# A macaron decoder trunk: the third conv group's products ahead of the scores, its taps behind the groups' maxima, the output projection begun between the last groups

## The chip, the cores and the metric

The kernel runs on one core of one Trainium2 chip. The metric is the device time of one execution in microseconds (us). The engines are TensorE (PE; PEld is its weight load), VectorE (DVE), ScalarE (ACT), GpSimd (POOL) and SyncE (SP, which issues the loads). Matmuls write to PSUM, of which the kernel has eight banks of 128 x 512 floats: three under the tag `mm`, one `cf`, two `po`, two `pt`.

## The reference

Two layers over 512 tokens of width 1024, all in float32. Each layer is a half-step SwiGLU (inner width 2816), a mixer, a second half-step SwiGLU and a norm. The change is in the mixer alone:

```python
n = rms_norm(h, mix_norm[l])
p = n @ w_in[l]
u_conv, q, k, v, q_mem = jnp.split(p, splits, axis=-1)
y_conv = conv_module(u_conv, ...)   # GLU, causal depthwise conv of 31 taps, LayerNorm, silu: 384 channels
y_swa = sliding_window_attention(q, k, v, sinks)   # 6 heads, window 128, blocks of 128, learned sinks
y_mem = memory_attention(qm, mk, mv)   # 4 heads over 256 memory tokens
y = jnp.concatenate([y_conv, y_swa, y_mem], axis=-1)
h = h + y @ w_out[l]
```

q, k and qm are normed a head; q and k are rotated.

## The kernel before, in words

Activations lie with channels on the partitions, as tiles of 128 x 512. Every large product is made of three matmuls in a rounded format, hi*hi + lo*hi + hi*lo (`mm3`, lines 174 to 176), so each weight tile is first split into a rounded half `hi` and the rest `lo`. `weights` does that in one of two ways. With VectorE: ACT copies the loaded tile `raw` to `hi` (L143) and VectorE subtracts (L144). With POOL (`split_by_dma`): ACT makes `hi` (L148) and `-hi` (L149), and an accumulating DMA that POOL issues adds the weights to it from memory (L150). There are three `raw` buffers and four pairs of `whi` and `wlo`; `spare()` gives another place, the pair of a gated tile.

The mixer of a layer, in the order of the string ORDER:

- `conv_half(c, i)`, steps c00 to c21: the products of conv group c (three groups of 128 channels), i = 0 the values and i = 1 the gates. VectorE scales them by R, the spread of the token norms (L665, L668), ACT takes the sigmoid (L669), VectorE multiplies (L670) into `ypad`.
- `queries(t)`, q0 to q3, one block of 128 tokens each, with norms and rotation on ACT (L684, L537), POOL (L689) and VectorE; `query_columns(t)`, Q0 to Q3, transposes them. `values(t)`, v0 to v3, makes the values and the memory queries, which ACT copies out (L711, L713) and squares (L537); `value_columns(t)`, V0 to V3, transposes the memory queries.
- `attention`, step a, works through ten groups (GROUPS) of up to three head pairs, "r" for memory heads, "w" for window heads. `scored` makes the scores of a group on PE (L741 the mask, L747) and their maxima on VectorE (L751 or L765), and scales these to a bias (L752 or L766 and L767). `turned` takes the exponentials on ACT (L777), transposes them on PE (L783) and copies them back (L785); `weighted` multiplies by the values on PE (L794); `scaled` divides (L803 to L808); `attended` transposes the result (L817) and splits it. The scores of group n + 1 are issued ahead of the exponentials of group n.
- `taps(c)`, t0 to t2: 31 VectorE instructions a group (L871 once, L874 thirty times), one after another on the same 128 x 512 sums. They come last in ORDER, and the scheduler puts them where VectorE is free.
- `swish`, step s: POOL adds the three groups' sums (L880, L881), PE makes their mean (L883), VectorE subtracts it (L886), ACT squares, PE adds up the squares (L200), VectorE and POOL take the root (L206, L191), PE spreads it over the partitions (L213), and norm and silu follow (L891, L892).
- The output projection: eight tiles of 128 output channels, each from five tiles of attention rows (three of the window heads, two of the memory heads) and three of conv rows. First the five of each, 15 matmuls a tile, then the conv rows, 9 a tile, whose weights are called `ours`; h is updated (L922).

Each engine runs its instructions in order. What that order is, a scheduler decides ahead of time: it takes instructions as they are written here, and picks by its own model of time what an engine does next. `queued()` binds a PE instruction behind the PE instruction that was last put in `tail`, so that PE's order within the mixer is the written one; `tc.issue_after` does the same behind any instruction named. Neither is a wait at run time.

Of the kernel before, what the change touches and what calls it, by code (L numbers as in the profile page):

```python
# [18 lines left out]
P = 128  # L19
# [26 lines left out]

ORDER = "c00 c01 q0 c10 q1 c11 Q0 q2 v0 Q1 q3 v1 Q2 v2 v3 Q3 V0 V1 c20 V2 V3 a t0 t1 t2 s"

# [13 lines left out]
def trunk(ctx: ExitStack, tc: tile.TileContext, xT, memT, pos, w1a, w3a, w2a, w1b, w3b, w2b,  # L62
# [549 lines left out]
    def mixer(l, x, st, last):  # L612
# [28 lines left out]
        def spare():  # L641

            return tuple(z.rearrange("p i s -> p (i s)") for z in gated_pair())

        def conv_half(c, i):
            nonlocal R
            ps = bank([P, S], "po") if c == 2 else mm()
            with queued():
                project(ps, weights(wconv[l, c, i], 1024, V if c + i < 2 else G, spare() if c == 2 else None), x)
            if c == 0:  # L650
                with queued():
                    if i == 0:
                        V.tensor_copy(rc, rms_cols(st, D))
                    else:
                        R = kept(spread(rc), "R", V)
            halves.append((c, i, ps))
            while halves and R is not None:
                gate(*halves.pop(0))
# [17 lines left out]
        def queries(t):  # L676
# [19 lines left out]
            per_head(q[:, CCH:], rq[:, t, NH:], 2)  # L696

        def query_columns(t):
            with queued():
                pt = to_columns(qT[:, :, blk(t)], query[t // 2][:, t % 2], 4)  # L700
            A.activation(kT[:, blk(t)], pt[:, CC, :], AF.Copy, scale=HD**-0.5)
# [29 lines left out]
        def scored(kind, pairs):  # L731
# [17 lines left out]
            if not masked:  # L749
                for i in range(2):  # L750
                    V.tensor_reduce(out=nmr[:, b, i], in_=pp[i], axis=AX.X, op=ALU.max)  # L751
                V.scalar_tensor_tensor(out=nmr[:, b], in0=nmr[:, b], scalar=-1.0, in1=by_half(rm[:, b, :]), op0=ALU.mult, op1=ALU.mult)  # L752
                return pp, W
# [12 lines left out]
            V.scalar_tensor_tensor(out=at_(nmw), in0=at_(nmw), scalar=-1.0, in1=rr, op0=ALU.mult, op1=ALU.mult)  # L766
            V.tensor_tensor(out=at_(nmw), in0=at_(nmw), in1=per(nsinks), op=ALU.min)  # L767
            G.tensor_tensor(out=at_(esw), in0=at_(nmw), in1=per(sinks), op=ALU.add)
            return pp, W

        def turned(kind, b, c, scores, W):
# [3 lines left out]
            for i in range(2):  # L775
                n = 2 * c + i
                A.activation(pr[:, i, 0:W], scores[i], AF.Exp, bias=nm[:, b, i, c : c + 1], scale=rr[:, b, n : n + 1])  # L777
            nk = W // P
# [32 lines left out]
        def attended(kind, b, z):  # L811
# [7 lines left out]
            while c < n:  # L819
# [6 lines left out]
        GROUPS = (("r", (0, 0), (0, 1)), ("r", (1, 0), (1, 1)), ("w", (0, 0), (0, 1), (0, 2)), ("w", (1, 0), (1, 1)), ("w", (2, 0), (2, 1)),  # L826
                  ("w", (1, 2), (2, 2)), ("r", (2, 0), (2, 1)), ("w", (3, 0), (3, 1)), ("w", (3, 2)), ("r", (3, 0), (3, 1)))

        def attention():
# [17 lines left out]

            s = scored(GROUPS[0][0], GROUPS[0][1:])
            conv_half(2, 1)
            yy.extend([gated_pair() for _ in range(KD // 2)][::-1])  # L850
            y.extend(at(p, ALL, i, ALL) for p in yy for i in range(2))
            for n, (kind, *pairs) in enumerate(GROUPS):
                ready = list(done)
                done.clear()
                nxt_s = None
                if n + 1 < len(GROUPS):
                    nxt_s = scored(GROUPS[n + 1][0], GROUPS[n + 1][1:])
                for z, (b, c) in enumerate(pairs):
                    x = turned(kind, b, c, [ps[:, z, :] for ps in s[0]], s[1])
                    close()  # L860
                    late = (kind, b, c, *x)
                s = nxt_s
                for r in ready:
                    attended(*r)
            close()
            for r in done:
                attended(*r)


        def taps(c):  # L870
            V.tensor_scalar(out=cv[:, c, :], in0=ypad[:, c, 0:S], scalar1=conv_w[:, c, 0:1], scalar2=conv_b[:, c : c + 1],  # L871
                            op0=ALU.mult, op1=ALU.add)
            for j in range(1, TAPS):
                V.scalar_tensor_tensor(out=cv[:, c, :], in0=ypad[:, c, j : j + S], scalar=conv_w[:, c, j : j + 1],  # L874
                                       in1=cv[:, c, :], op0=ALU.mult, op1=ALU.add)

# [17 lines left out]

        for step in ORDER.split():
            f = {"c": conv_half, "q": queries, "Q": query_columns, "v": values, "V": value_columns, "a": attention, "t": taps,
                 "s": swish}[step[0]]
            f(*map(int, step[1:]))


        oo = []
        for d in range(KD):
            w = weights(wout[l, d, :, CCH:], 640, G if d < 4 else V)
            ps = bank([P, S], ("mm", "mm", "mm", "cf", "po", "po", "pt", "pt")[d])
            for n in range(5):
                mm3(ps, at(w, ALL, blk(n)), y[CC + n], n == 0, False)
            oo.append(ps)

# [141 lines left out]
```

## Time and profile before

| what | us |
|---|---|
| three runs, median | 1813.62 |
| lowest and highest of them | 1808.96 and 1815.8 |
| the profiled execution | 1811.26 |
| its span in the profile | 1809.1 |
| PE busy in the span | 1767.9 |
| VectorE busy | 1281.7 |
| ACT busy | 897.4 |
| layer 0's mixer, first conv gate to first output product | 397.0 to 507.4 |
| layer 1's, the same | 1290.7 to 1399.9 |

Times inside a profile are counted from the start of its span. A row of the timeline has the start, the duration, the engine, the line, the operation, output and inputs, and in brackets the idle time of the engine just before, with what ended it. A row of a stretch has the busy time of each engine in it with the count of instructions, the clock that PE was granted (1.00 is full), the busy share of the DMA engines, and GB/s.

### The profile page before, as it was taken

The page shows a single profiled execution, that of the slowest core. Times are in us where ns is not written, and L with a number is a line of the kernel's source. Part 1 is how long each engine was busy: PE and PEld are TensorE (multiplying, and loading weights), DVE is VectorE, ACT ScalarE, POOL GpSimd, SP SyncE. Part 2 cuts the span into 40 slices and gives each one's busy share as a digit, 9 for nine tenths or more (in the row PEclk, how much of TensorE's full clock was granted, in tenths as well). Part 3 has the DMA queues.
Part 4 walks back from the last instruction along what each step waited for, and adds up shares of the span by engine and source line. Part 5 has one row for each costly group of instructions (what it writes and reads, how often), then busy time and mean ns, then how long its engine had stood idle before and what let it go on. Part 6 is the DMA issues. An engine that isn't in the chain of part 4 may idle for free.

```text
span 1809.1 us, 28077 instructions
## 1 busy us (share of the span) xinstructions
PE 1767.9 (98%) x10996; PEld 1585.8 (88%) x10996; DVE 1281.7 (71%) x1896; ACT 897.4 (50%) x1357; POOL 189.0 (10%) x207
## 2 busy tenths in 40 slices
PE   8999999999899999999999999999989999999997
PEld 6989999888688989898888898988877889898986
DVE  7969666569957857575678685766698567675755
ACT  5546444464655535353655463535456645453532
POOL 3001000025001000000010010000340010000000
PEclk9999999999899999999999999999999999999998
DMA  9466655275039456465556465643640666474622
GB/s 274 107 168 173 177 131 150 55 203 114 2 104 206 111 143 172 135 167 138 155 137 156 145 174 142 172 120 94 162 104 1 182 139 162 129 182 121 168 80 82
DMA packets 93589, 250.44 MB, mean 138 GB/s; under 512 B 9617, under 2 KB 11921, under 8 KB 93457
## 3 DMA queue, kind: packets, MB, share of 16 engines
q1 hardware_dynamic: 77040, 190.45, 34.9%
q0 software_dynamic: 16416, 58.20, 17.8%
q8 instruction: 86, 1.41, 0.3%
q14 instruction: 47, 0.38, 0.1%
HBM read 246.52 MB, written 2.10 MB: 137 GB/s over the span
## 4 chain that ended last, share of the span: by engine, by line
PE 79%; DVE 11%; issue 6%; ACT 2%; DMA 2%; SPq 0%; POOLq 0%; DVEq 0%; POOL 0%; ACTq 0%
PE mm L174 10%; PE mm L176 10%; PE mm L175 10%; PE po L176 9%; PE po L174 9%; PE po L175 9%; PE pt L174 6%; PE pt L175 6%; PE pt L176 6%; DVE there L874 6%; DMA raw<-in_wvm 1%; DVE wlo L144 1%; PE po L794 1%; DVE nmw L765 1%; ACT uu L777 0%
## 5 line engine op out<-in xcount | busy, mean ns | idle before, releaser
L143 ACT ACTIVATE whi<-raw 128x1024 fp32r<-128x1024 f32 (+3 forms) x360 | 337.9, 941 | 487.0 <-PE mm L175 235.7
L144 DVE TENSOR_TENSOR wlo<-raw,whi 128x1024 fp32r<-128x1024 f32 (+3 forms) x352 | 380.1, 1081 | 145.1 <-ACT whi L143 143.6
L175 PE MATMUL mm<-glo,whi 128*128 128x512 f32 x752 | 293.6, 391 | 0.0
L174 PE MATMUL mm<-ghi,whi 128*128 128x512 f32 x752 | 290.5, 391 | 0.7 <-ACT ghi L143 0.7
L176 PE MATMUL mm<-ghi,wlo 128*128 128x512 f32 x734 | 285.6, 389 | 0.0
L176 PE MATMUL po<-mh,wlo 128*128 128x256 f32 x864 | 244.6, 283 | 1.1 <-DVE wlo L144 1.1
L174 PE MATMUL po<-mh,whi 128*128 128x256 f32 x864 | 244.7, 283 | 0.2 <-ACT part L386 0.2
L175 PE MATMUL po<-ml,whi 128*128 128x256 f32 x864 | 244.5, 283 | 0.0
L176 PE MATMUL pt<-xhi,wlo 128*128 128x256 f32 x864 | 244.0, 283 | 0.0
L175 PE MATMUL pt<-xlo,whi 128*128 128x256 f32 x864 | 243.9, 283 | 0.0
L174 PE MATMUL pt<-xhi,whi 128*128 128x256 f32 x864 | 243.0, 283 | 0.3 <-ACT xhi L143 0.3
L464 DVE SCALAR_TENSOR_TENSOR h<-mm,h 128x512 f32<-128x512 f32 x128 | 87.7, 688 | 138.1 <-PE mm L176 138.1
L174 PEld LDWEIGHTS mm<-ghi,whi 128*128 128x128 f32 x752 | 141.2, 188 | 30.3 <-ACT ghi L143 1.2
L176 PEld LDWEIGHTS po<-mh,wlo 128*128 128x128 f32 x864 | 165.8, 192 | 1.3 <-DVE wlo L144 1.3
L174 PEld LDWEIGHTS po<-mh,whi 128*128 128x128 f32 x864 | 165.8, 192 | 1.2 <-ACT part L386 0.4
L175 PEld LDWEIGHTS pt<-xlo,whi 128*128 128x128 f32 x864 | 165.7, 192 | 0.8
L175 PEld LDWEIGHTS po<-ml,whi 128*128 128x128 f32 x864 | 165.8, 192 | 0.6
L174 PEld LDWEIGHTS pt<-xhi,whi 128*128 128x128 f32 x864 | 165.1, 192 | 1.4 <-ACT xhi L143 0.5
L175 PEld LDWEIGHTS mm<-glo,whi 128*128 128x128 f32 x752 | 141.3, 188 | 28.3 <-issue 0.5
L176 PEld LDWEIGHTS pt<-xhi,wlo 128*128 128x128 f32 x864 | 165.6, 192 | 0.0
L176 PEld LDWEIGHTS mm<-ghi,wlo 128*128 128x128 f32 x734 | 137.8, 188 | 29.0 <-issue 0.5
L874 DVE SCALAR_TENSOR_TENSOR there<-ypad,par,there 128x512 f32<-128x512 f32 x180 | 135.5, 764 | 1.4
(314 smaller groups left out, 3305.9 us busy)
## 6 DMA issues: line engine op xcount, KB each, us to landing
raw<-in_w2a SPq DMA_DIRECT2D x48, 384.0 KB, 3.6
raw<-in_w2b SPq DMA_DIRECT2D x48, 384.0 KB, 3.5
raw<-in_w1b SPq DMA_DIRECT2D x26, 512.0 KB, 3.7
raw<-in_w3b SPq DMA_DIRECT2D x26, 512.0 KB, 3.7
raw<-in_w1a SPq DMA_DIRECT2D x25, 512.0 KB, 3.7
raw<-in_w3a SPq DMA_DIRECT2D x25, 512.0 KB, 3.7
wsum<-in_w1a SPq DMA_DIRECT2D x18, 512.0 KB, 4.4
wsum<-in_w3a SPq DMA_DIRECT2D x18, 512.0 KB, 4.3
```

The lines of the kernel that those rows point to most:

```text
L143: A.activation(hi, x, AF.Copy)
L144: on.tensor_tensor(out=lo, in0=x, in1=hi.bitcast(F32), op=ALU.subtract)
L174: T.matmul(ps, a[0], b[0], start=first, stop=False, **more)
L175: T.matmul(ps, a[0], b[1], start=False, stop=False, **more)
L176: tail[0] = T.matmul(ps, a[1], b[0], start=False, stop=last, **more)
L464: added = V.scalar_tensor_tensor(out=h[:, d, :], in0=ps, scalar=0.5, in1=h[:, d, :], op0=ALU.mult, op1=ALU.add)
L765: V.tensor_reduce(out=each(nmw, i), in_=pp[i], axis=AX.X, op=ALU.max)
L794: tail[0] = T.matmul(po[:, 2 * c + i, :], ptb[:, i, j, :], v, start=(j == 0), stop=(j == nk - 1))
L874: V.scalar_tensor_tensor(out=cv[:, c, :], in0=ypad[:, c, j : j + S], scalar=conv_w[:, c, j : j + 1], in1=cv[:, c, :], op0=ALU.mult, op1=AL ...
```

## The change

ORDER becomes `c00 c01 q0 c10 q1 c11 Q0 q2 q3 Q1 c20 c21 Q2 v0 Q3 v1 V0 V1 g0 g1 v2 v3 V2 a t0 t1 t2 s`. The third conv group's products (c20, c21) come ahead of the values and of all scores; the scores of groups 0 and 1 (g0, g1, the new function `begin`) come ahead of v2 and v3; V3 moves into the first group. The weights of v0 to v3 lie in spare pairs, two of the four split by POOL. The taps from the 58th on (EARLY) are bound behind the last step of the groups' maxima, by the counts in LATER. The last three groups change places: the memory heads of block 3 come ahead of the window heads of block 3, and one pair of window heads comes last. The output projection is cut in two functions: `out_weights(d)`, called for the first two tiles ahead of the groups and for the next two inside groups 3 and 5, and `out_rows(d, rows)`, called with the rows of the memory heads (MEMORY) for the first three tiles around the last step of the attention, and with those of the window heads (OWN) after `swish`. `out_rows` issues under `queued()`. The `ours` weights are split by ACT and accumulating DMAs of POOL.

```diff
-ORDER = "c00 c01 q0 c10 q1 c11 Q0 q2 v0 Q1 q3 v1 Q2 v2 v3 Q3 V0 V1 c20 V2 V3 a t0 t1 t2 s"
+ORDER = "c00 c01 q0 c10 q1 c11 Q0 q2 q3 Q1 c20 c21 Q2 v0 Q3 v1 V0 V1 g0 g1 v2 v3 V2 a t0 t1 t2 s"
+EARLY = 58
+LATER = (4, 4, 3, 3, 3, 3, 3, 3, 3, 3)
...
         def conv_half(c, i):
-            ps = bank([P, S], "po") if c == 2 else mm()
+            ps = mm()
-                project(ps, weights(wconv[l, c, i], 1024, V if c + i < 2 else G, spare() if c == 2 else None), x)
+                project(ps, weights(wconv[l, c, i], 1024, V if c + i < 2 else G), x)
...
         def values(t):
-                ww["v"] = [weights(wvm[l, i], 768, V) for i in range(4)]
-            ps = mm()
+                ww["v"] = [weights(wvm[l, i], 768, V if i < 2 else G, spare()) for i in range(4)]
+            ps = mm() if t < 2 else bank([P, S], "po")
...
+        def begin(n):
+            begun[n] = scored(GROUPS[n][0], GROUPS[n][1:])
...
-            s = scored(GROUPS[0][0], GROUPS[0][1:])
-            conv_half(2, 1)
+            for d in range(2):
+                with tc.issue_after(keyed[2].ins):
+                    out_weights(d)
...
+                if final:
+                    for r in ready:
+                        attended(*r)
+                    ready = []
+                elif n + 1 not in begun:
+                    begin(n + 1)
+                if n in (3, 5):
+                    with tc.issue_after(raised[GROUPS[n - 1][0], *GROUPS[n - 1][-1]].ins):
+                        out_weights(len(out_w))
...
+            out_rows(0, MEMORY)
             close()
+            out_rows(1, MEMORY)
+            out_rows(2, MEMORY)
             for r in done:
                 attended(*r)
...
+        OWN, MEMORY = range(CC), range(CC, 5)
+        def out_rows(d, rows):
+            if d == len(oo):
+                oo.append(bank([P, S], ("mm", "mm", "mm", "cf", "po", "po", "pt", "pt")[d]))
+            with queued():
+                for n in rows:
+                    mm3(oo[d], at(out_w[d], ALL, blk(n)), y[CC + n], n == CC, False)
...
             for j in range(1, TAPS):
+                n = c * TAPS + j - EARLY
+                group = sum(n >= sum(LATER[:g]) for g in range(1, len(LATER)))
+                with tc.issue_after(biased[group].ins) if n >= 0 else nullcontext():
...
         for d in range(KD):
+            if d == len(out_w):
+                out_weights(d)
+            out_rows(d, OWN if d < 3 else (*MEMORY, *OWN))
...
-            split(own[0], own[1], raw[:, 0 : 2 * CCH], V)
+            A.activation(own[0], raw[:, 0 : 2 * CCH], AF.Copy)
+            A.activation(own[1], raw[:, 0 : 2 * CCH], AF.Copy, scale=-1.0)
+            for j in range(2):
+                G.dma_start(own[1][:, blk(j, CCH)], wout[l, 2 * i + j, :, 0:CCH], accum_op=ALU.add)
```

How the order of instructions moves is shown at three places of layer 0; numbers behind a name tell tiles apart. Line numbers in the new kernel are higher.

The first is ACT ahead of its first sigmoid. Before, it converts the tiles of c10 (whi_3908), of c11 (whi_3981, wlo_3982) and the first two of the values' weights (128x768):

```order
L143 ACTIVATE whi_3908<-raw_3910 128x1024
L148 ACTIVATE whi_3981<-raw_3983 128x1024
L149 ACTIVATE wlo_3982<-raw_3983 128x1024
L143 ACTIVATE whi_4063<-raw_4065 128x768
L143 ACTIVATE whi_4069<-raw_4071 128x768
L669 ACT_TABLE_LOAD
L669 ACTIVATE aux2_3744<-aux2_3744 128x512
```

Now the tiles of c20 (whi_4112) and c21 (whi_4145) stand there, two copies each:

```order
L151 ACTIVATE whi_3981<-raw_3983 128x1024
L152 ACTIVATE wlo_3982<-raw_3983 128x1024
L151 ACTIVATE whi_4112<-raw_4114 128x1024
L152 ACTIVATE wlo_4113<-raw_4114 128x1024
L151 ACTIVATE whi_4145<-raw_4147 128x1024
L152 ACTIVATE wlo_4146<-raw_4147 128x1024
L675 ACT_TABLE_LOAD
L675 ACTIVATE aux2_3744<-aux2_3744 128x512
```

The values' weights have moved behind the copies of q2.

The second is ACT from its first exponentials to the first copy of turned exponentials (aux0). Before, the sigmoid of c2 stands between them, with table loads:

```order
L777 ACTIVATE uu_3745<-mm_4335,nmr_3754,rm_3751 128x256
L669 ACT_TABLE_LOAD
L669 ACTIVATE aux2_3744<-aux2_3744 128x512
L785 ACTIVATE aux0_3742<-pt_4397 128x512
L785 ACTIVATE aux0_3742<-pt_4405 128x512
L777 ACT_TABLE_LOAD
```

Now the second group's first exponentials and the copies of v2 (po_4313) and v3 (po_4347) stand there:

```order
L786 ACTIVATE pr_3748<-mm_4304,nmr_3754,rm_3751 128x256
L786 ACTIVATE pr_3748<-cf_4305,nmr_3754,rm_3751 128x256
L719 ACTIVATE here_3739<-po_4313,rc_3749 128x2x64
L721 ACTIVATE aux0_3742<-po_4313,rc_3749 128x256
L540 ACTIVATE hsq_4340<-po_4313,rc_3749 128x256
L719 ACTIVATE here_3739<-po_4347,rc_3749 128x2x64
L721 ACTIVATE aux0_3742<-po_4347,rc_3749 128x256
L540 ACTIVATE hsq_4374<-po_4347,rc_3749 128x256
L575 ACTIVATE there_3740<-pt_4381 128x2x128
L786 ACTIVATE uu_3745<-mm_4304,nmr_3754,rm_3751 128x256
L794 ACTIVATE aux0_3742<-pt_4409 128x512
```

The sigmoid of c2 has gone to a place ahead of all exponentials, and the tables change once less often there and back.

The third is PE at the end of the attention. Before, the mean of the conv sums (onesq) stands among the products of the first three output tiles (mm_4957, mm_4980, mm_5003), as the sums of squares and the spread do further on:

```order
L174 MATMUL mm_4957<-ghi_4380,whi_4950 128x512
L174 MATMUL mm_4980<-ghi_4380,whi_4973 128x512
L174 MATMUL mm_5003<-ghi_4380,whi_4996 128x512
L883 MATMUL pt_4906<-aux2_3744,onesq_104 128x512
L175 MATMUL mm_4957<-glo_4381,whi_4950 128x512
L176 MATMUL mm_4957<-ghi_4380,wlo_4951 128x512
```

Now (output tiles mm_4824, mm_4840, mm_4847) they follow one another:

```order
L179 MATMUL mm_4847<-ghi_4399,wlo_4537 128x512
L826 MATMUL pt_4854<-cst_96,aux1_3743 128x128 x3
L928 MATMUL pt_4957<-aux2_3744,onesq_104 128x512
L203 MATMUL cf_4969<-onesq_104,st_4960 128x1 x4
L203 MATMUL cf_4969<-onesq_104,sq_4967 128x1 x4
L216 MATMUL pt_4982<-cst_96,rsq4_4980 128x128 x4
L177 MATMUL mm_4824<-ghi_4403,whi_4385 128x512
```

The 18 products with the memory heads' rows end ahead of them, and every other product of the projection comes behind the spread (L216).

More of the change, by code (lines that the diff above doesn't have):

```diff
@@ L776, in turned @@
                 n = 2 * c + i
-                A.activation(pr[:, i, 0:W], scores[i], AF.Exp, bias=nm[:, b, i, c : c + 1], scale=rr[:, b, n : n + 1])
+                raised[kind, b, c] = A.activation(pr[:, i, 0:W], scores[i], AF.Exp, bias=nm[:, b, i, c : c + 1], scale=rr[:, b, n : n + 1])
             nk = W // P
@@ L873, in taps @@
             for j in range(1, TAPS):
-                V.scalar_tensor_tensor(out=cv[:, c, :], in0=ypad[:, c, j : j + S], scalar=conv_w[:, c, j : j + 1],
-                                       in1=cv[:, c, :], op0=ALU.mult, op1=ALU.add)
+                n = c * TAPS + j - EARLY
+                group = sum(n >= sum(LATER[:g]) for g in range(1, len(LATER)))
+                with tc.issue_after(biased[group].ins) if n >= 0 else nullcontext():
+                    V.scalar_tensor_tensor(out=cv[:, c, :], in0=ypad[:, c, j : j + S], scalar=conv_w[:, c, j : j + 1],
+                                           in1=cv[:, c, :], op0=ALU.mult, op1=ALU.add)
         def swish():
@@ L895, in mixer @@
         for step in ORDER.split():
-            f = {"c": conv_half, "q": queries, "Q": query_columns, "v": values, "V": value_columns, "a": attention, "t": taps,
-                 "s": swish}[step[0]]
+            f = {"c": conv_half, "q": queries, "Q": query_columns, "v": values, "V": value_columns, "g": begin, "a": attention,
+                 "t": taps, "s": swish}[step[0]]
             f(*map(int, step[1:]))
-        oo = []
         for d in range(KD):
[L903 to L907, printed above, removed]
+            if d == len(out_w):
+                out_weights(d)
+            out_rows(d, OWN if d < 3 else (*MEMORY, *OWN))
         more = res.tile([P, 4, 2 * CCH], F32R, tag="nsh", name="whi")
```

24 lines of the change are left out of this document (15 added, 9 removed).

## The prediction

> **What bounds the kernel now.** The page comes first: the run as a whole stands on PE.
>
> ```profile
> span 1809.1 us, 28077 instructions
> PE 1767.9 (98%) x10996; PEld 1585.8 (88%) x10996; DVE 1281.7 (71%) x1896; ACT 897.4 (50%) x1357; POOL 189.0 (10%) x207
> ```
>
> That is an average. The change touches only the mixer, once a layer, so I took the busy time by stretches of layer 0's mixer. After the span of a stretch come PE, PEld, DVE, ACT and POOL, then the granted clock and DMA.
>
> ```profile
> 375.00:380.00 5.00, 4.29 (x19) 2.84 (x17) 2.71 (x4) 5.00 (x8) 1.64 (x2) 1.00 1.04 256
> 380.00:385.00 5.00, 5.00 (x19) 4.15 (x20) 0.91 (x2) 1.74 (x2) 1.93 (x2) 0.66 1.06 274
> 460.00:465.00 5.00, 3.55 (x18) 3.11 (x20) 3.29 (x6) 4.96 (x9) 0.07 (x1) 0.50 0.00 0
> 465.00:470.00 5.00, 5.00 (x33) 4.78 (x31) 3.91 (x10) 1.39 (x4) 0.19 (x1) 0.57 0.00 0
> ...
> 396.98:499.22 102.24, 95.20 (x554) 79.86 (x554) 98.01 (x188) 55.19 (x113) 35.22 (x37) 0.95 0.25 55
> 507.40:555.00 47.60, 47.57 (x221) 39.40 (x222) 28.13 (x43) 28.36 (x41) 4.22 (x5) 1.00 0.63 175
> ```
>
> Three limits follow one another. From the first conv gate (396.98) to the last tap (499.22) VectorE is busy for 98.0 of 102.2 us, so it is the bound there. PE's time between 460 and 470 is at half clock. From 507.4 on PE has no gap at all: the output projection hides everything else.
>
> The timeline of PE shows where it waits in the attention; the bracket is the idle time just before a row.
>
> ```profile
> 461.45 1.97 PE L794 MATMUL po<-mvn,aux 128*128 128x65 f32 x8 [1.77 <-ACT aux L785]
> ...
> 484.91 0.89 PE L783 MATMUL pt<-cst,pr 128*128 128x128 f32 x4 [0.42 <-ACT pr L777]
> 487.23 0.66 PE L783 MATMUL pt<-cst,uu 128*128 128x128 f32 x4 [0.59 <-ACT aux L785]
> 495.03 0.89 PE L783 MATMUL pt<-cst,uu 128*128 128x128 f32 x4 [0.80 <-ACT uu L777]
> 497.16 0.66 PE L783 MATMUL pt<-cst,uu 128*128 128x128 f32 x4 [0.40 <-ACT aux L785]
> 502.70 0.89 PE L783 MATMUL pt<-cst,uu 128*128 128x128 f32 x4 [0.93 <-ACT uu L777]
> 507.43 0.96 PE L174 MATMUL mm<-ghi,whi 128*128 128x512 f32 x3 [0.37 <-ACT ghi L143]
> ```
>
> The last row is the first product of the output projection. The six waits from 484.91 on sum to 3.5 us; PE waits for exponentials whose maxima VectorE reached late, behind taps.
>
> **The change part by part.** *The start of the taps.* ACT runs in order, and before the first sigmoid it converts weights.
>
> ```profile
> 386.93 1.06 ACT L148 ACTIVATE whi<-raw 128x1024 fp32r<-128x1024 f32 x1 [2.71 <-DMA raw<-in_wconv]
> 387.90 1.04 ACT L149 ACTIVATE wlo<-raw 128x1024 fp32r<-128x1024 f32 x1
> 390.53 0.85 ACT L143 ACTIVATE whi<-raw 128x768 fp32r<-128x768 f32 x1 [1.60 <-DMA raw<-in_wvm]
> 393.25 0.85 ACT L143 ACTIVATE whi<-raw 128x768 fp32r<-128x768 f32 x1 [1.87 <-DMA raw<-in_wvm]
> 394.11 1.28 ACT L669 ACT_TABLE_LOAD   x1
> 396.32 0.63 ACT L669 ACTIVATE aux<-aux 128x512 f32<-128x512 f32 x1 [0.92 <-DVE aux L668]
> ```
>
> Two wvm tiles of 384 KB land 2.72 us apart (390.53, 393.25), with the DMA engines full (share 1.04 to 1.06 above). In their place now stand two wconv tiles of 512 KB: 3.63 us each at that rate, so 2 x 0.9 = 1.8 us more. Each takes two copies and not one; only the last tile's count, 2 x 0.97 - 0.85 = 1.1. The 0.92 us for which the sigmoid then waited for VectorE goes, since VectorE no longer has wvm splits ahead of R. Sum +2.0: the taps start at 399.0. PE doesn't wait for it: its next products (q1, c11) stand on banks that VectorE frees with R, ahead of the sigmoid.
>
> *The first maxima.*
>
> ```profile
> 452.97 0.68 DVE L751 TENSOR_REDUCE nmr<-mm 128x2 f32<-128x512 f32 x1
> 455.49 0.15 DVE L752 SCALAR_TENSOR_TENSOR nmr<-nmr,rm 128x4 f32<-128x4 f32 x1
> 457.04 1.93 ACT L777 ACTIVATE uu<-mm,nmr,rm 128x256 f32<-128x256 f32 x4
> 460.82 1.07 ACT L785 ACTIVATE aux<-pt 128x512 f32<-128x512 f32 x2
> L874 DVE SCALAR_TENSOR_TENSOR there<-ypad,par,there 128x512 f32<-128x512 f32 x90 | 67.7, 763 | 0.7
> ```
>
> ```profile
> 420.83 0.37 ACT L711 ACTIVATE here<-cf,rc 128x128 f32<-128x128 f32 x1 [2.98 <-PE cf L176]
> 421.10 0.47 ACT L713 ACTIVATE aux<-cf,rc 128x256 f32<-128x256 f32 x1
> 421.45 0.48 ACT L537 ACTIVATE hsq<-cf,rc 128x256 f32<-128x256 f32 x1
> ```
>
> The row of L874 groups the 90 taps of the stretch; the last three are the copies that one `values` step makes on ACT. By the order, VectorE has 52 tap rows ahead of the first maximum and not 56 (4 x 0.763 = 3.0 less), the sums of squares of v2 and v3 no longer (some 0.8, half as wide as the maximum of 0.68) and two more gate steps of c2 (1.2, as wide as it): -2.6. With the late start, 452.97 + 2.0 - 2.6 = 452.4; the first bias comes 2.5 later as now, 454.9, and the exponentials at 456.3, 0.7 earlier than now. But the copy that PE waits for (460.82) moves back on ACT: the second sigmoid and two table loads go, and ahead of it come two more exponentials (0.9), the six copies of v2 and v3 (2.0 by the starts of the rows at 420.83 to 421.45 and the next 0.36), a copy of queries and an exponential (0.8). It begins 1.9 + 0.9 + 2.0 + 0.8 = 5.6 us behind the first exponential and not 3.8. So 1.8 later less 0.7 earlier, rounded down, **+1.0** at group 2's scores. That PE has the scores ready some us earlier buys nothing, since VectorE comes to the maxima no sooner. Bounds: -1.0 (the taps start no later) to +3.0 (they start twice as late).
>
> *The groups.* From group 2 on VectorE has three taps a group where it had four, and the maxima stand ahead of them; 0.7 us a group is what it was late by. The six waits go: **-3.5**. Bounds -3.5 to 0. The two weight tiles that ACT now converts inside groups 3 and 5 (1.3 us each) lie in its idle time (55.2 us busy of 102.2).
>
> *The tail.* This is the term against the change. In the order of PE the conv's mean, its sums of squares and the spread of its root now stand in a row, and the products with the window heads' rows (OWN) wait behind the spread, because `out_rows` issues under `queued()`. Before, products stood between. What one step of that chain takes:
>
> ```profile
> 499.37 1.27 POOL L881 TENSOR_TENSOR aux<-aux,there 128x512 f32<-128x512 f32 x1 [0.86 <-DVE there L874]
> 510.51 1.02 PE L883 MATMUL pt<-aux,onesq 128*128 128x512 f32 x2
> 511.57 1.89 DVE L886 SCALAR_TENSOR_TENSOR there<-pt,there 128x512 f32<-128x512 f32 x3 [2.08 <-PE pt L883]
> 512.89 1.23 ACT L234 ACTIVATE sq<-there 128x512 f32<-128x512 f32 x2
> 513.56 0.69 DVE L246 TENSOR_TENSOR st<-st,sq 128x512 f32<-128x512 f32 x1
> 519.48 1.03 PE L200 MATMUL cf<-onesq,sq 128*128 128x1 f32 x8
> 520.55 0.16 DVE L206 TENSOR_SCALAR ms<-cf 128x4 f32<-128x4 f32 x1 [2.35 <-PE cf L200]
> 520.79 1.03 POOL L191 TENSOR_TENSOR rsq<-ms,nhalf 128x4 f32<-128x4 f32 x1 [20.16 <-DVE ms L206]
> ```
>
> From the end of the mean (511.53) to the sum of squares ready (514.25) are 2.7 us, and 0.3 for the last heads' split that VectorE now has in between: PE stands for 3.0. From the end of its sums (520.51) past L206 and L191 to 521.82, and some 0.2 to get there: 1.5. **+4.5** a layer; bounds 4.0 and 5.5. The 18 products taken ahead run in both versions and gain nothing by themselves.
>
> *The clock.* Does a pause bring half clock? Rows 460 and 465 lose (0.50 + 0.43) x 5 = 4.65 us, behind waits of some 3 us; row 380 loses 0.34 x 5 = 1.7, behind a row with 0.71 us idle. So 0 to 4.65. I take **+1.7**: row 380 is the nearer, because dense products follow it, as they follow the pauses here, while more waits follow row 460. The Trainium skill (TensorE: Matmul & The Clock Gate, Part 1: The HAM clock gate) has the clock halve after an idle window of about 3.4 us and return after a busy one; by it the pauses would cost one or two windows, an estimate of 1.7 to 3.4, and the layer's sum would be 3.7 to 5.4. The trace agrees only in part, as row 380 shows half clock without an idle window.
>
> *At nothing:* the own weights' low halves by DMA (eight accumulating DMAs on POOL, two ACT copies a tile for one VectorE split): PE is gapless from 507.4 to 555.0, and the first is needed eight output tiles after the spread, 102 products of 0.227, 23 us (the window's 47.6 us, less some 4.0 for the matmuls of mean, sums and spread, over 192 products); each us beyond that cover would be a us. Two of the wvm splits move to POOL, behind the rotations of q2 and q3 in its queue; they are needed 10 us later.
>
> *Sum a layer:* 1.0 - 3.5 + 4.5 + 1.7 = +3.7. Both layers have the same order, and layer 1 the same rows within some 0.2 us, with half clock there too:
>
> ```profile
> 1355.00:1360.00 5.00, 4.87 (x25) 4.21 (x26) 2.94 (x7) 3.78 (x7) 0.00 (x0) 0.50 0.02 3
> ```
>
> So +7.4. The profiled execution took 1811.26 (span 1809.1 and 2.2 around it), 2.4 below the median of 1813.62. 1811.26 + 7.4 = 1818.7, which is **1821.0** against that median.
>
> **Rivals.** *1, faster: the first groups run free.* If the exponentials of groups 0 and 1 do run under v2 and v3, the stall at 461.45 and the half clock go, and only VectorE bounds the attention: 399.0, 98.0 of work, and 3.1 for the last group's maxima and splits that now precede the last tap (five rows of 0.3 to 0.7), gives 500.1; POOL's add 1.3: the mean at 501.4, where my sum has 507.4 + 1.0 - 3.5 + 4.1 (18 products of 0.227) = 509.0. That is 7.6 less, -3.9 a layer, -5.6 without the clock's 1.7: 1802.4 to 1805.8. For it: scores come early. Against: VectorE is busy 98 of 102 us and the first maximum is behind 52 taps.
>
> *2, slower: the clock stays at half behind the pauses* for as long as at the first groups, 4.65 and not 1.7. It decides where the clock is not back by the time that some 8 of OWN's 27 products are done, which is what a loss of 1.7 pays for. 3.7 + 3.0 = 6.7 a layer: 1827.0. For it: rows 460 and 465; against: row 375's gap cost 1.7.
>
> *3, the tail is not idle:* other work fills PE between mean and spread. The order leaves none there; then pauses and half clock go, a layer is at -2.5 and the kernel at 1808.6.
>
> **How the numbers follow.** A measurement can tell about 0.5%, 9.1 us: below 1804.6 is faster, above 1822.7 slower. Forecast 0.60, with its own range 1814 to 1826, of which 0.17 lies above 1822.7; rival 1 0.15 (0.13 of it below 1804.6); rival 2 0.20, slower; rival 3 0.05, no change. Faster 0.13, same 0.50, slower 0.37. The range from 1804 to 1832 leaves out most of rival 1 and the end of rival 2.
>
> **What would show it.** In the changed profile: first sigmoid near 398.4 and not 396.32; the first maximum near 452.4; no PE wait above 0.3 between group 2's scores and the 18 products; two PE pauses of 3.0 and 1.5 around the sums of squares; half clock behind them; gapless products after. I am wrong if PE's first-group wait is gone (rival 1), if the pauses are absent (rival 3), or if PE waits for own weights.

## The result: 1.5% slower, and the profile after

The changed kernel takes 1840.58 us (median of 4 runs, 1837.32 to 1841.22) against 1812.56 of the kernel before: ratio 1.0151, 95% interval 1.0128 to 1.0175. That is 28 us, where 7.4 were forecast, and above the range's end of 1832. The page of the changed kernel begins:

```profile
span 1839.2 us, 28077 instructions
PE 1783.1 (97%) x10996; PEld 1595.8 (87%) x10996; DVE 1270.8 (69%) x1884; ACT 898.5 (49%) x1365; POOL 208.4 (11%) x227
```

PE still fills the span, and is busy 15 us longer with the same 10996 instructions: these ran at half clock for longer. The other half of the 30 us is new idle time. Where both lie, four stretches of a mixer show. They are bounded by a wait of PE at the mixer's start (its row begins at 378.32 before and at 378.27 now), the first product with the window heads' values (group 2), the end of the conv's mean, the first product of the next half-step, and that half-step's first spread:

| stretch, us before and after | layer 0 | layer 1 |
|---|---|---|
| mixer's start to group 2 | 94.7, 97.8 (+3.1) | 93.7, 93.8 (+0.1) |
| group 2 to the end of the mean | 38.5, 37.4 (-1.1) | 38.4, 37.4 (-1.0) |
| mean to the next half-step's first product | 43.5, 50.8 (+7.3) | 43.5, 51.1 (+7.7) |
| from there to its spread | 11.8, 20.2 (+8.4) | 11.8, 16.3 (+4.5) |

The last two stretches carry it. In the changed kernel's layer 0 they read (after the span come PE, PEld, DVE, ACT, POOL, granted clock, DMA share):

```profile
513.42:564.20 50.78, 46.51 (x198) 39.13 (x199) 16.33 (x25) 25.86 (x36) 10.72 (x12) 0.90 0.61 158
564.20:584.44 20.24, 16.79 (x57) 11.96 (x56) 10.72 (x18) 8.47 (x14) 3.64 (x4) 0.83 0.91 218
```

The same two stretches in the kernel before:

```profile
511.53:554.99 43.46, 43.46 (x205) 36.31 (x204) 26.98 (x39) 27.58 (x39) 4.21 (x5) 1.00 0.69 192
554.99:566.83 11.84, 11.84 (x58) 9.90 (x57) 3.59 (x7) 3.62 (x6) 3.15 (x4) 1.00 0.91 184
```

Before, PE had no gap and full clock in both. Now it stands 4.27 and 3.45 us, at a mean clock of 0.90 and 0.83. Its timeline shows the waits; the bracket is the idle time just before a row:

```profile
458.14 0.44 PE L573 MATMUL pt<-cst,aux 128*128 128x128 f32 x2 [2.32 <-ACT aux L721]
...
485.17 0.66 PE L792 MATMUL pt<-cst,uu 128*128 128x128 f32 x4 [0.39 <-ACT aux L794]
...
504.75 0.41 PE L826 MATMUL pt<-cst,aux 128*128 128x128 f32 x2 [0.59 <-DVE aux L817]
505.65 0.66 PE L792 MATMUL pt<-cst,uu 128*128 128x128 f32 x4 [0.49 <-DVE glo L147]
...
516.33 1.56 PE L203 MATMUL cf<-onesq,st 128*128 128x1 f32 x8 [2.91 <-DVE st L249]
...
520.95 2.08 PE L216 MATMUL pt<-cst,rsq 128*128 128x128 f32 x8 [1.36 <-POOL rsq L194]
```

```profile
567.36 0.50 PE L178 MATMUL mm<-xlo,whi 128*128 128x512 f32 x1 [0.73 <-DVE xlo L157]
...
569.22 0.50 PE L178 MATMUL mm<-xlo,whi 128*128 128x512 f32 x1 [0.90 <-DVE xlo L157]
...
570.48 0.50 PE L178 MATMUL mm<-xlo,whi 128*128 128x512 f32 x1 [0.30 <-DVE xlo L157]
```

The pauses of 2.91 and 1.36 are those of the forecast. The last fence is what it had not seen: the next half-step's products wait six times in layer 0, five times for the remainders `xlo` of the updated h and once for a rounded half `xhi`.

How long the clock stays down behind the pauses, stretch by stretch:

```profile
513.28:516.70 3.42, 0.51 (x5) 0.38 (x4) 2.81 (x5) 2.16 (x4) 0.00 (x0) 1.00 0.00 0
516.70:520.11 3.41, 2.89 (x15) 2.80 (x14) 0.16 (x1) 0.00 (x0) 0.24 (x1) 0.50 0.00 0
520.11:523.52 3.41, 2.57 (x10) 2.47 (x11) 0.00 (x0) 0.45 (x1) 0.79 (x1) 0.50 0.01 2
523.52:526.93 3.41, 3.41 (x9) 2.64 (x9) 1.29 (x2) 3.38 (x6) 0.00 (x0) 0.50 0.00 0
526.93:530.35 3.42, 3.42 (x16) 2.83 (x16) 3.30 (x5) 2.74 (x6) 0.00 (x0) 1.00 0.00 0
```

One stretch with PE busy 0.51 of 3.42 us is followed by three at half clock, 10.2 us. PE was busy for 8.9 us of these, so half clock cost about 4.4 us. The edges are chosen to fit: the half clock begins and ends on them.

Why `xlo` is late, VectorE's rows of the changed kernel show:

```profile
551.81 1.23 DVE L147 TENSOR_TENSOR wlo<-raw,whi 128x1024 fp32r<-128x1024 f32 x1 [14.55 <-ACT whi L146]
554.05 1.22 DVE L147 TENSOR_TENSOR wlo<-raw,whi 128x1024 fp32r<-128x1024 f32 x1 [1.02 <-ACT whi L146]
555.20 1.28 DVE L967 TENSOR_TENSOR h<-mm,h 128x512 f32<-128x512 f32 x2
559.80 0.75 DVE L157 SCALAR_TENSOR_TENSOR xlo<-h,gn,xhi 128x512 fp32r<-128x512 f32 x1 [3.32 <-ACT xhi L156]
```

and those of the kernel before:

```profile
534.01 1.23 DVE L144 TENSOR_TENSOR wlo<-raw,whi 128x1024 fp32r<-128x1024 f32 x1 [2.83 <-ACT whi L143]
...
536.96 1.22 DVE L144 TENSOR_TENSOR wlo<-raw,whi 128x1024 fp32r<-128x1024 f32 x1
...
543.86 1.88 DVE L922 TENSOR_TENSOR h<-mm,h 128x512 f32<-128x512 f32 x3 [2.83 <-PE mm L176]
545.66 1.58 DVE L154 SCALAR_TENSOR_TENSOR xlo<-h,gn,xhi 128x512 fp32r<-128x512 f32 x2
```

In VectorE's order the splits of the next half-step's first two weight tiles stand ahead of the updates of h, in both kernels. Before, the second of them ended at 538.18, 5.7 us ahead of the first update, which waited for PE. Now VectorE stands 14.55 us for the first of them, and the update begins at 555.20. PE's last product of the first output tile began at 549.70, so the update is some 5 us later than PE alone would make it. SyncE's queue tells why those weights come late, first the kernel after, then before:

```profile
484.38 45.66 SPq L104 DMA_DIRECT2D raw<-in_wout  x2
530.44 6.16 SPq L958 DMA_DIRECT2D raw<-in_wout  x6
...
538.22 0.45 SPq L104 DMA_DIRECT2D raw<-in_w1b  x1
```

```profile
518.23 8.32 SPq L916 DMA_DIRECT2D raw<-in_wout  x8
526.76 0.33 SPq L101 DMA_DIRECT2D raw<-in_w1b  x1
```

The queue stands until 530 for one of three `raw` buffers. A buffer is free when ACT has copied its tile and VectorE has subtracted. Here these are the tiles of output 4 and on; ACT's first copy in the kernel after, then before:

```profile
527.44 0.72 ACT L146 ACTIVATE whi<-raw 128x640 fp32r<-128x640 f32 x1
```

```profile
515.47 0.74 ACT L143 ACTIVATE whi<-raw 128x640 fp32r<-128x640 f32 x1 [1.35 <-PE mm L175]
```

These copies need a pair of `whi` and `wlo` that output tiles 0 to 3 hold. Before, ACT waited for PE's products with tile 0 until 515.47. Now these products begin behind the spread, at 522.68, and the copy runs 12 us later. (In ACT's order it stands behind the copy of the spread and the first silu, from 523.07 on; the next copy, at 528.82, waits 0.65 us for PE's products.) So, by this reading, the binding holds back weights, their buffers, the next weights, and through VectorE's order the updates of h.

### The profile page after: what moved, and what is told of

Its sections match the earlier page's. It is cut to its first block, busy times and chain, and to the rows that moved or that the text cites. A ratio compares the mean times of both kernels' runs of the same rounds, so it can differ in the third digit from the quotient of the medians.

```text
span 1839.2 us, 28077 instructions
## 1 busy us (share of the span) xinstructions
PE 1783.1 (97%) x10996; PEld 1595.8 (87%) x10996; DVE 1270.8 (69%) x1884; ACT 898.5 (49%) x1365; POOL 208.4 (11%) x227
## 4 chain that ended last, share of the span: by engine, by line
PE 71%; DVE 11%; issue 8%; DMA 5%; ACT 4%; POOL 0%; SPq 0%; POOLq 0%; DVEq 0%; ACTq 0%
PE mm L177 10%; PE mm L178 10%; PE mm L179 9%; PE po L179 8%; PE po L177 8%; PE po L178 8%; PE pt L177 5%; PE pt L178 5%; PE pt L179 5%; DVE there L919 4%; DMA raw<-in_wconv 1%; DMA wsum<-in_w1b 1%; DVE wlo L147 1%; DMA raw<-in_wout 1%; DVE xlo L157 1%
## 5 line engine op out<-in xcount | busy, mean ns | idle before, releaser
L146 ACT ACTIVATE whi<-raw 128x1024 fp32r<-128x1024 f32 (+3 forms) x344 | 324.4, 946 | 454.5 <-PE mm L178 234.3
L147 DVE TENSOR_TENSOR wlo<-raw,whi 128x1024 fp32r<-128x1024 f32 (+3 forms) x344 | 372.6, 1085 | 156.2 <-ACT whi L146 155.2
L177 PE MATMUL mm<-ghi,whi 128*128 128x512 f32 x752 | 294.2, 393 | 0.0
```

The lines of the kernel that those rows point to most:

```text
L146: A.activation(hi, x, AF.Copy)
L147: on.tensor_tensor(out=lo, in0=x, in1=hi.bitcast(F32), op=ALU.subtract)
L177: T.matmul(ps, a[0], b[0], start=first, stop=False, **more)
```

## The experiments

The theory (A) was that the binding of the products (`queued()` in `out_rows`) does all of this; the rival (B) that the late start comes from the conv rows' weights, read from memory twice.

**The binding taken away** (e1_free):

```diff
-            with queued():
+            with queued() if bound else nullcontext():
...
-            out_rows(d, OWN if d < 3 else (*MEMORY, *OWN))
+            out_rows(d, OWN if d < 3 else (*MEMORY, *OWN), False)
```

> The changed kernel, but the products behind swish are not bound behind the spread of the root; those with the memory heads' rows ahead of it stay bound. Theory A (the binding alone costs the tail and, through it, the start of the next half-step: the weight pairs of the first output tiles come free late, so the next weights are split and loaded late): the pauses of 2.91 and 1.36 around the sums of squares go, the half clock behind them too, and the six waits at the start of the next half-step with them; 1840.6 less (7.3 + 8.4) less (7.7 + 4.5) is about 1813, at most 1816. Theory B (the start of the next half-step is late because the conv rows' weights are now read twice from memory and split by ACT and POOL): only the tail comes back, 1840.6 less 15.0, about 1825.5.

Measured 1812.6, ratio to before 0.9998 (0.9985 to 1.0011). The stretch from mean to next half-step in layer 0:

```profile
511.75:556.02 44.27, 42.87 (x199) 35.03 (x198) 22.88 (x35) 30.69 (x44) 10.74 (x12) 1.00 0.79 207
```

44.27 and not 50.78, at full clock; the loads of w1b begin at 526.45, and PE has no wait at the next half-step. The whole loss hangs on the binding: without it the rest of the change, double reading included, is worth nothing measurable.

**The second reading taken away**, the binding kept (e2_ours_dve):

```diff
-            A.activation(own[0], raw[:, 0 : 2 * CCH], AF.Copy)
-            A.activation(own[1], raw[:, 0 : 2 * CCH], AF.Copy, scale=-1.0)
-            for j in range(2):
-                G.dma_start(own[1][:, blk(j, CCH)], wout[l, 2 * i + j, :, 0:CCH], accum_op=ALU.add)
+            split(own[0], own[1], raw[:, 0 : 2 * CCH], V)
```

> The changed kernel, but the conv rows' weights are split by ACT and VectorE as before, without the accumulating DMAs. Theory A (binding): the tail stays as it is and the start of the next half-step stays late, since the loads still begin near 530; 1837 to 1841. Theory B (double reading): the next half-step's weights land some 5 us or more earlier, its six waits of 3.5 and 2.7 us and what follows them go; 1840.6 less (8.4 + 4.5), about 1828.

Measured 1835.9 (1.0125, 1.0101 to 1.0148): near A. That is 4.7 below the changed kernel, but the two intervals overlap, so this run alone doesn't show that the double reading costs that much (e5 below does). The waits at the start are down to 0.81 and 1.87. What it does to the queue, from the DMA issues between 500 and 570 of the changed kernel (KB each, us to landing):

```profile
raw<-in_w1b SPq DMA_DIRECT2D x4, 512.0 KB, 6.5
...
whi<-in_wout POOLq DMA_DIRECT2D x8, 192.0 KB, 9.7
```

In e2 the first row falls to 5.4; the kernel before has 4.2.

**The binding alone, in the kernel before** (e3_before_bound):

```diff
-            for n in range(5):
-                mm3(ps, at(w, ALL, blk(n)), y[CC + n], n == 0, False)
+            with queued():
+                for n in range(5):
+                    mm3(ps, at(w, ALL, blk(n)), y[CC + n], n == 0, False)
```

> The kernel before with one thing added: the output projection's 120 products with the attention's rows are bound behind the spread of the root. Theory A (the binding is the whole loss): two pauses of about 3.0 and 1.5 with half clock behind them, 7 a layer, and a late start of the next half-step, 8.4 and 4.5: 1812.6 + 27, about 1838 to 1841. Theory B (the loss needs the new weights' path): the tail's share only, 1812.6 + 14.5, about 1827.

Measured 1833.1 (1.0108, 1.0093 to 1.0124), 9.8 a layer, between the theories. PE pauses 2.77 and 1.37, and the clock is at half for 10.2 us, as in both layers of every kernel with the bound products and unfilled pauses (the changed one, e2, e3, e12, e14). The next half-step has no wait at all, the last `xlo` coming 3.3 and 4.7 us behind its first product. So the binding by itself costs the tail, and for the late start other edits of the changed kernel must be there. The double reading is likely one of them, as e2's shorter waits suggest. Another could be the 18 products taken ahead: from the spread to the next half-step are 47.0 us here and 43.3 in the changed kernel. That was not tested.

**The pauses filled** with matmuls that the kernel doesn't need (e6_filled):

```diff
+            over = bank([P, S], "po")
+            fill(3)
...
+            with queued():
+                v = rms_cols(st, CCH)
+            fill(2)
```

> The changed kernel with matmuls into an unused bank in the two pauses of PE, three 128x512 ones behind the mean and two behind the sums of squares (work that the kernel doesn't need). They leave the chain as long as it is, or 0.5 longer. If half clock is the price of PE's idling: no half clock behind the spread, and 3.0 a layer come back less 0.5, about 1835.5, and perhaps some of the late start. If half clock there has another cause: it stays, 1840 to 1842.

Measured 1825.95 (1.0069, 1.005 to 1.0089): 14.6 back, not 5. PE's rows, and the clock (third number from the end):

```profile
512.43 2.74 PE L934 MATMUL po<-aux,onesq 128*128 128x512 f32 x6
515.50 1.05 PE L203 MATMUL cf<-onesq,st 128*128 128x1 f32 x8 [0.33 <-DVE st L249]
```

```profile
515.00:520.00 5.00, 4.67 (x30) 3.54 (x29) 0.61 (x2) 0.18 (x1) 1.03 (x1) 1.00 0.00 0
520.00:525.00 5.00, 5.00 (x24) 4.13 (x23) 2.00 (x3) 4.77 (x7) 0.00 (x0) 1.00 0.01 2
```

With no useful work more, half clock is gone in layer 0 (in layer 1 3.4 us of it are left): the stretch from mean to next half-step falls by 3.9 and 2.6. So half clock there was the price of idling. The start gave back 2.9 and 3.3 more: its waits fell from 3.45 to 1.51 and from 2.73 to 0.49.

**What holds the start.** First ACT's copies of the next half-step's third and fourth weight tile moved behind parts of h (e12_late_copies):

```diff
+            if f == 1 and w13[0] is w1b:
+                behind.append(put[2 + 3 * i])
...
+        with tc.issue_after(behind[-1].ins) if behind else nullcontext():
```

> The changed kernel with its bound products as they are; ACT converts the next half-step's third and fourth weight tile behind its roundings of h's tiles 2 and 5 (xhi) and not ahead of the first. Nothing else moves. Theory A (the next half-step starts late because the remainders of h, xlo, come late, and the first one waits for ACT behind weights that land late): the first xlo comes 2 to 3 us sooner, the waits of 3.5 and 2.7 us fall below 1.5, the half clock of layer 0 there goes; 1840.6 less 5 to 9, 1832 to 1836. Theory B (PE would wait for these weights or for VectorE's pace all the same): 1838 to 1842.

Measured 1838.7 (1.0134, 1.0111 to 1.0157), not told apart from the changed kernel. The waits fell to 1.95 and 2.05, though the first `xlo` came 3 us sooner against the update: the expectation looked at the wrong end. Then the first two tiles too, on ACT and VectorE (e14_h_first):

```diff
-            if f == 1 and w13[0] is w1b:
-                behind.append(put[2 + 3 * i])
+            if f < 2 and w13[0] is w1b:
+                behind.append(put[(1, 3, 4, 6)[2 * f + i]])
```

> The changed kernel with its bound products as they are; ACT and VectorE convert the next half-step's first four weight tiles behind the roundings and remainders (xhi, xlo) of h's tiles 1, 3, 4 and 6, and not ahead of the first update of h. Theory A (in e12_late_copies the updates of h still stood behind two splits on VectorE whose weights land late; PE waits according to when the last remainder is ready): the first update of h comes near 548 and not 553 to 555, the last remainder at most 5 us behind the next half-step's first product, its waits and the half clock there go: 1840.6 less 9 to 13, 1828 to 1832. Theory B (the next half-step's weights themselves are what is late): PE waits for them in place of the remainders, 1836 to 1842.

Measured 1826.0 (1.0064, 1.0044 to 1.0085), 15 below the changed kernel and 2 below theory A's range, with the pauses as they were:

```profile
545.38 0.69 DVE L976 TENSOR_TENSOR h<-mm,h 128x512 f32<-128x512 f32 x1 [12.88 <-PE mm L184]
546.87 0.75 DVE L162 SCALAR_TENSOR_TENSOR xlo<-h,gn,xhi 128x512 fp32r<-128x512 f32 x1 [0.80 <-ACT xhi L161]
...
550.88 1.22 DVE L151 TENSOR_TENSOR wlo<-raw,whi 128x1024 fp32r<-128x1024 f32 x1
```

The update comes when PE has the tile, the split stands behind, and PE waits nowhere at the start: the stretch from the next half-step's first product to its spread is back at 11.8 us in both layers. So it was the order on VectorE and ACT, with late weights in front. What PE's wait follows is the end of the eighth `xlo`, counted from the next half-step's first product:

| kernel, layer | last `xlo` ends behind it | PE idle |
|---|---|---|
| changed, 0 and 1 | 9.95, 9.18 | 3.45, 2.73 |
| e12, 1 and 0 | 9.37, 8.76 | 2.05, 1.95 |
| e6, 0 and 1 | 7.18, 5.87 | 1.51, 0.49 |
| e14, 1 and 0 | 4.70, 4.55 | 0, 0 |
| before, both | 2.83 | 0 |

PE takes the first tile's eight parts in 24 matmuls of 0.227, 5.4 us. Most of what `xlo` ends behind that is waited for (4.5 us against a wait of 3.45 in the first row), and where it ends sooner there is no wait.

**The taps' binding** taken from the free kernel (e4_free_taps):

```diff
-EARLY = 58
+EARLY = 200
```

> The kernel of e1_free (1812.6), with the taps not bound behind the groups' maxima. If the binding of the taps is worth the 3.5 a layer that the prediction gave it, the six waits in the groups come back: about 1819.6. If it is worth what the stretch from group 2 to the mean lost (1.1 a layer): about 1814.8. If the order of the scheduler is as good: 1812.6.

Measured 1842.25 (1.0145, 1.0123 to 1.0167): 27 us above e1_free by the ratios, and no expectation is near. In its layer 1:

```profile
1379.97 0.82 PE L792 MATMUL pt<-cst,uu 128*128 128x128 f32 x2 [4.04 <-ACT uu L786]
```

All taps run ahead of the later maxima (the last ends at 488.43 and not 506.36). The new order needs this binding; by e1 it gains nothing over the kernel before, which has no such binding.

**Repairs.** e5_free_ours_dve is e1_free with the edit of e2. e7_v2_first is e1_free with the exponentials behind ACT's copies of v2:

```diff
-                raised[kind, b, c] = A.activation(pr[:, i, 0:W], ...
+                with tc.issue_after(copied[2].ins):
+                    x = A.activation(pr[:, i, 0:W], ...
```

e9_placed has that edit, and keeps the binding but writes the products into `swish`; e10_placed2 places them again and has the edit of e2:

```diff
+            tail[0] = T.matmul(pm, onesq, s1, start=True, stop=True)
+            out_rows(0, OWN)
+            out_rows(1, OWN)
...
+            with queued():
+                v = rms_cols(st, CCH)
+            out_rows(2, OWN)
+            with queued():
+                RL = kept(spread(v), "RL")
```

e13_v2_ours is e7 with the edit of e2; e11_filled2 is e10 with two matmuls that the kernel doesn't need ahead of V3's transposes.

> The kernel of e1_free, with the conv rows' weights split by ACT and VectorE as before. If double reading costs only where the loads begin late: 1811 to 1814, as e1_free. If it costs everywhere, as in the bound kernel (4.7 of 28): about 1808.

Measured 1807.8 (0.9968, 0.9952 to 0.9984), just clear of e1_free's interval: the double reading costs 5 us with free products too. Between 500 and 570 its loads of w1b (512 KB) land in 4.3 us, where e1_free's take 6.4.

> The kernel of e1_free, with the exponentials bound behind ACT's copies of v2, so that ACT does these in the 7.8 us in which it waits for the first bias. Theory A (PE's wait of 2.3 to 2.4 ahead of the transposes of v2, and the half clock behind it, come from that order on ACT): the wait goes, half clock too, and 2.4 + 1.5 a layer at least come back: 1803 to 1806. Theory B (VectorE bounds the attention, and PE waits for the exponentials in its place): 1811 to 1814, half clock as it is.

Measured 1807.6 (0.9974, 0.996 to 0.9988), between the theories. ACT, in the changed kernel and then in e7:

```profile
453.33 1.28 ACT L786 ACT_TABLE_LOAD   x1 [7.80 <-DVE nmr L760]
```

```profile
449.66 0.37 ACT L719 ACTIVATE here<-po,rc 128x128 f32<-128x128 f32 x1 [6.17 <-PE po L179]
```

ACT makes the copies of v2 inside its wait for the first bias, but PE's wait of 2.4 becomes 1.8 and 0.6 at the next bank and copy, and two windows at half clock, 6.8 us, stay in each layer.

> The changed kernel with the exponentials behind the copies of v2 as in e7_v2_first, and its bound products placed by hand: the window heads' rows of tiles 0 and 1 (18 products) between mean and sums of squares, those of tile 2 (9) between sums and spread, all others behind the spread. 18 x 0.227 = 4.1 and 9 x 0.227 = 2.0 cover the waits of 2.91 and 1.36, and the root is ready sooner than in e1_free, where PE waited 1.4 and 1.2 for conv rows. Theory A: e7_v2_first less 2 to 3, 1800 to 1804. If the conv rows were not late in e1_free for want of the spread: as e7_v2_first.

> The kernel of e7_v2_first with the conv rows' weights split by ACT and VectorE: the three repairs together with the scheduler's own placing of the products. e7_v2_first was 5 below e1_free and e5_free_ours_dve 5 below it; if both act on different stretches they add up: about 1803. If both are one (the half clock that a run happens to take): 1807.

> The kernel of e9_placed with the conv rows' weights split by ACT and VectorE, and the products placed again: the memory heads' rows of tile 2 and the window heads' of tile 0 (15 products, 3.4 us) between mean and sums, those of tile 1 (9) between sums and spread. The wait of 1.38 for the last window heads' split goes, and the last remainder of h lies 2 us sooner or more before its use: e9_placed less 2 x (1.4 + 1.1), about 1802. As e13_v2_ours if the scheduler's placing is as good.

> The kernel of e10_placed2 with two 128x512 matmuls into an unused bank (work that the kernel doesn't need) in the wait of 1.8 us ahead of the transposes of v3. If the half clock of the first groups comes from PE's idling: it is gone in both layers, and some 3 a layer come back: 1795 to 1799. If VectorE bounds the groups however fast PE is: half clock gone, time as e10_placed2. If the half clock has another cause: it stays.

Measured: e9 1807.5 (0.9963, 0.995 to 0.9976), e13 1805.2 (0.9964, 0.995 to 0.9977), e10 1807.8 (0.9978, 0.9964 to 0.9991), e11 1809.5 (0.9981, 0.9968 to 0.9994). All beat the kernel before by 0.2 to 0.4%; none is told apart from another, nor from e5 and e7, so the further gains that were expected of e9, e10 and e11 did not come. e13 has the lowest median, and it leaves the placing of the products behind `swish` to the scheduler. Filling the wait of 1.8 in e11 left the others, of 0.60 and 1.55:

```profile
455.29 1.88 PE L729 MATMUL po<-R,onesq 128*128 128x512 f32 x4
...
467.27 1.81 PE L810 MATMUL po<-mvn,aux 128*128 128x65 f32 x8 [1.55 <-ACT aux L801]
```

Half clock stayed too, two windows in each layer. Whether that comes of the waits that are left or of something else is open.

## Why the prediction was wrong, point by point

*At nothing: wrong, and the largest miss.* The step said that PE has no gap from 507.4 to 555.0 and needs the first own weights only 23 us after the spread. That nearly held: conv rows began at 547.88 without a wait, but in layer 1 the last pair of own weights came late:

```profile
1469.97 0.47 PE L179 MATMUL pt<-ghi,whi 128*128 128x512 f32 x1 [0.48 <-ACT whi L151]
```

The profile names ACT, but what this product reads for the first time is the low half of the seventh tile's own weights. POOL issued its accumulating DMAs at 1458.40, and in layer 1 such a DMA takes 11.0 us to land (median). By the prediction's own sign (PE waits for own weights) the step was wrong here too, by 0.5 us.

The failed step is larger: the prediction took the gapless row of the kernel before (507.40:555.00) as cover that the changed kernel would still have. What it left out is who stands behind those weights: the `raw` buffers, the next half-step's loads, and on VectorE two splits ahead of the updates of h. That cost 8.4 and 4.5 us, priced at nothing. e1 shows that it goes with the binding, e14 that it lies in the order behind late weights, and e3 that the binding alone doesn't bring it about; which of the other edits do so, beside the double reading, stays open.

*The tail: right.* 4.5 forecast, 2.91 + 1.36 = 4.27 measured, in both layers.

*The clock: mechanism right, size wrong.* 1.7 forecast. The stretch from mean to next half-step grew 7.3 and 7.7, although six more products (18 and not 12, 1.4 us) now lie ahead of the mean. Less the pauses, and layer 1's 0.5 for own weights, that is 4.4 and 4.3. Rival 2's 4.65 was near the price, and the choice of row 380 as the nearer one was the failed step: no dense products follow the first pause, only the small sums and a second pause until 520.95. By the Trainium skill's rule (TensorE: Matmul & The Clock Gate, Part 1: The HAM clock gate), that the clock halves after an idle window and returns after a busy one, the estimate was at most 3.4; the trace agrees on the windows of 3.41 us, but here three were spent at half clock behind a single one in which PE was mostly idle. PE was busy for 2.89, 2.57 and 3.41 us of the three; so the clock came back behind the first window without a pause.

*The groups: too large.* -3.5 forecast. Waits of 0.39, 0.59 and 0.49 and one of 0.19 remain, and the stretch to the mean, cleared of the same 1.4, is 2.5 and 2.4 shorter.

*The first groups: +1.0 forecast, +3.1 and +0.1 measured; the size right but for the clock, partly by luck.* The maxima came sooner than reckoned:

```profile
391.66 1.06 ACT L151 ACTIVATE whi<-raw 128x1024 fp32r<-128x1024 f32 x1 [2.61 <-DMA raw<-in_wconv]
...
393.57 1.04 ACT L151 ACTIVATE whi<-raw 128x1024 fp32r<-128x1024 f32 x1
...
396.87 0.63 ACT L675 ACTIVATE aux<-aux 128x512 f32<-128x512 f32 x1
```

```profile
450.64 1.28 DVE L759 TENSOR_REDUCE nmr<-mm 128x2 f32<-128x512 f32 x2
```

First sigmoid 396.87, not 398.4: c21's tile (393.57) had landed by the time that c20's copies ended, so ACT waited for the loads once and not twice. First maximum 450.64, not 452.4. But ACT's copies of v2 and v3 behind the exponentials, which the forecast saw on ACT, stop PE earlier than it said, at V2's transposes (2.32). The difference between the layers is half clock: the stretch holds 17.1 us of it in layer 0 and 6.8 in layer 1, behind waits of nearly the same length; before, it held 13.7 and 10.2. Half of PE's busy time in these windows is 8.1 and 3.1 us now, and was 5.9 and 4.3. Without it the term is about +0.9 and +1.3, an estimate from these figures. That it comes so near the forecast is in part luck, as maxima and stop both came out otherwise. It is also one execution's: in the profiles of e1, e2, e6, e12 and e14, whose instructions are the same here, the stretch takes 93.4 to 98.0 us.

*The sum.* 3.7 a layer forecast. Measured: 3.1 - 2.5 + 4.3 + 4.4 + 8.4 = 17.7 in layer 0 and 0.1 - 2.4 + 4.3 + 4.3 + 0.5 + 4.5 = 11.3 in layer 1. With rival 2's clock the forecast would have been 1827.0, inside its range; the late start, in no rival, put the time outside. Rival 1 and rival 3 did not occur.

## What to carry to other kernels

To hold products back is to hold back everything that they release: follow weight buffers, then loads, then the splits that stand first in another engine's order, as far as the next stage's first product. Work whose order is left to the scheduler can fill a chain of small steps; bind only what has to be bound, and put something independent between the links. A pause on PE is to be priced at its length and the half clock behind it, here 10.2 us of it, 4.4 us of time, for pauses of 4.3.

## What the runs showed of the hardware

The half clock comes in whole windows of 3.41 us, on one grid through an execution that lies differently in another: one to five windows in a row were seen. The Trainium skill (TensorE: Matmul & The Clock Gate, Part 1: The HAM clock gate) calls the window free-running, and the trace agrees. How many windows follow is not set by the pause alone. Of two windows of the kernel before, the one with more idle time was not followed by half clock (rows 1 and 2 belong together, and rows 3 and 4):

```profile
377.18:380.59 3.41, 2.70 (x15) 1.62 (x13) 1.35 (x2) 3.41 (x5) 0.86 (x1) 1.00 1.04 253
380.59:384.01 3.42, 3.42 (x10) 2.75 (x10) 0.16 (x1) 0.94 (x2) 1.93 (x2) 0.50 1.06 274
438.62:442.04 3.42, 1.97 (x13) 1.47 (x12) 3.42 (x8) 3.42 (x10) 1.94 (x2) 1.00 0.74 202
442.04:445.45 3.41, 3.41 (x17) 2.83 (x18) 3.34 (x7) 1.64 (x4) 3.41 (x4) 1.00 0.92 174
```

And behind the first groups e9 lost none in layer 0 and five windows in layer 1, with waits of 1.78 and 0.60 us in both. Nor does a busy PE end it at once: in layer 0 of the changed kernel PE was busy through the last four of five windows at half clock (462.08 to 475.73). Executions of one kernel differ with this: e9's fastest, 1804.13, had a mean clock of 0.997, its slowest, 1813.86, one of 0.990. What sets the count stays open.
